# Inference step on one core: softmax factors in the turning matrix, compressed rows as one block, two landing places

## The chip, the cores and the metric

One Trainium2 chip, one of its cores. The metric is device microseconds (us) of one execution of the whole program; a kernel's time is the median of its runs. The profiled execution of the kernel before is one more execution of the same program, with its own time.

## The reference

One inference step of a small decoder with two trunk layers, for a prompt of 512 rows and a sample group of 8 rows (520 columns in the kernel). Layer 0 joins a state-space branch and an attention branch (16 heads of 64, two key groups) between one input projection and one output projection; layer 1 is a convolution module; behind each comes a feed-forward block. The change touches the attention of the prompt. For 128 queries and a head, three softmaxes are taken, each is scaled by a gate, and the weighted sums of the values are added:

```python
s_c = einsum('btghd,bngd->btghn', qg, kc)            # 31 compressed rows
p_c = masked_softmax(s_c, m_c);  o_c = einsum('btghn,bngd->btghd', p_c, vc)
p_s = masked_softmax(s_s, m_s);  o_s = einsum('btghnl,bgtnld->btghd', p_s, sel_v)   # selected blocks
p_w = masked_softmax(s_w, m_w);  o_w = einsum('btghs,bsgd->btghd', p_w, win_v)      # window
o = g[..., 0:1] * o_c + g[..., 1:2] * o_s + g[..., 2:3] * o_w
```

## The kernel before

Everything stands transposed: features on the 128 partitions, rows (tokens) along the free axis. Weights and activations are split into a high and a low fp32r part, and a product is three passes (mm3, L310): high by high, high by low, low by high. wload (L296) brings a weight tile of 128x1024 (512 KB) into a landing place, raw, by a DMA that SyncE issues; split (L292) makes its high part on ScalarE and its low part on VectorE, and the landing place is free again when the low part is made. The pool raw has three places, is opened once at the start (L264), and serves the whole program.

The mixer (L684) runs layer 0 in stages. First the projections of keys, values and queries and the whole attention of the sample group, with 10 of 40 tiles xz of the input projection for the state-space branch. Then the attention of the prompt: 16 steps (4 head groups hg of 4 heads, by 4 blocks b of 128 queries), between which the other 30 xz tiles are put. Then the scans of the four state-space groups, with the first 16 tiles of the output projection beside them, and at last the other 8 output tiles (wout(1, m)), which need the last scans' output.

A step of attention (L1106 to L1216) splits the queries into QS, makes the scores of the compressed rows (32 keys for each of the four heads, into pc) and their softmax, and for each head the scores over 128(b+1) keys twice (r = 0 the window, r = 1 the selected blocks), their maxima on VectorE and their exponentials on ScalarE, into pt. The sums give the factors mx[:, 2] (gate by reciprocal). L1174 to L1180 multiply each of the 8 exponentials of the step by its factor, in place: on VectorE, but r = 0 of b = 0 and b = 2 on ScalarE (ACT_NORM). Then turned (L1182) turns the weights: for each block of 128 keys and each r four transposes by the identity (L1186) into one PSUM tile pT of 512 columns, which is split into pth (ScalarE) and ptl (VectorE); two products of 512 columns by the block's values VB add into po (L1199, L1200). The compressed rows come last, as a block of 32 keys: four transposes of 32 columns, a split of 32x512, two products with VC. The tiles pT and po share three PSUM places (gen, L692); pth and ptl have two places each.

begin (L1653) closes layer 0: behind the last scan's pools (sp_, fx, ux, closed at L1446 to L1448) it opens the pools of what follows, h among them, which lie where the scan's tiles lay, and the last 8 output tiles use these pools and the landing places raw. The order of instructions on each engine is set by a planner from the program's order and its own estimate of durations; each engine works its list in that order.

## Time and profile before

| | us |
|---|---|
| median of 3 runs (lowest, highest) | 1958.77 (1958.25, 1962.19) |
| the profiled execution | 1961.67 |
| its span, first to last instruction | 1959.9 |
| attention of the prompt, first QS to the last sum, in the span | about 270 to 668 |
| last scan, boundary to the last 8 output tiles | about 845 to 905 |

In the profile, PE is TensorE's products and PEld its weight loads, which overlap; DVE is VectorE, ACT is ScalarE, POOL is GpSimd, SPq is SyncE's queue of DMA issues. A line of a group gives the kernel line, the engine, the operation, what it writes and reads, the tile shapes and how often it runs. PE's busy time counts pipelined products with modelled ends, so a product's own duration (about 0.27 us) is much longer than the distance to the next one; the rate of a run of products is read from starts. PEclk is the granted clock of TensorE as a share of 2.4 GHz.

### The profile page before, as it was taken

The page shows a single profiled execution, that of the slowest core. Times are in us where ns is not written, and L with a number is a line of the kernel's source. Part 1 is how long each engine was busy: PE and PEld are TensorE (multiplying, and loading weights), DVE is VectorE, ACT ScalarE, POOL GpSimd, SP SyncE. Part 2 cuts the span into 40 slices and gives each one's busy share as a digit, 9 for nine tenths or more (in the row PEclk, how much of TensorE's full clock was granted, in tenths as well). Part 3 has the DMA queues.
Part 4 walks back from the last instruction along what each step waited for, and adds up shares of the span by engine and source line. Part 5 has one row for each costly group of instructions (what it writes and reads, how often), then busy time and mean ns, then how long its engine had stood idle before and what let it go on. Part 6 is the DMA issues. An engine that isn't in the chain of part 4 may idle for free.

```text
span 1959.9 us, 38005 instructions
## 1 busy us (share of the span) xinstructions
PE 1835.2 (94%) x14449; PEld 1706.1 (87%) x14449; DVE 1415.3 (72%) x3385; ACT 974.4 (50%) x2093; POOL 189.5 (10%) x226
## 2 busy tenths in 40 slices
PE   6998889999998799998999999999989899999997
PEld 5997888988887588987999999998667789999997
DVE  5764768888887698968667766574786865666766
ACT  3223446676666577646555433355127755444433
POOL 0000021101000003130000211001111000000000
PEclk9999998999998799989999999999999999999999
DMA  8446254444321274543245433222433223444421
GB/s 296 114 140 197 76 190 130 149 138 129 126 90 57 92 243 136 157 143 100 87 143 165 132 105 109 87 81 53 119 107 119 87 87 116 122 119 120 148 62 49
DMA packets 125947, 240.90 MB, mean 123 GB/s; under 512 B 16499, under 2 KB 63236, under 8 KB 125444
## 3 DMA queue, kind: packets, MB, share of 16 engines
q1 hardware_dynamic: 120676, 221.45, 36.9%
q0 software_dynamic: 4000, 13.73, 2.2%
q10 hardware_dynamic: 1088, 3.29, 0.5%
q8 instruction: 114, 1.87, 0.4%
q14 instruction: 69, 0.57, 0.1%
HBM read 200.75 MB, written 30.88 MB: 118 GB/s over the span
## 4 chain that ended last, share of the span: by engine, by line
PE 43%; DVE 5%; ACT 3%; DMA 2%; issue 1%; SPq 0%; POOL 0%; DVEq 0%; ACTq 0%; POOLq 0%
PE up L312 8%; PE up L313 8%; PE up L314 8%; PE dn L312 4%; PE dn L313 4%; PE dn L314 4%; PE dn L624 2%; PE pw L312 1%; PE pw L313 1%; PE pw L314 1%; PE ns L333 1%; DMA raw_dn<-in_w_down 1%; DVE xf L385 1%; DVE h L387 1%; DVE facc L631 1%
## 5 line engine op out<-in xcount | busy, mean ns | idle before, releaser
L312 PE MATMUL dn<-gh,wh_dn 128*128 128x256 f32 (+1 forms) x704 | 198.0, 285 | 4.8 <-ACT gh L463 2.6
L314 PE MATMUL dn<-gh,wl_dn 128*128 128x256 f32 (+1 forms) x704 | 198.9, 284 | 0.0
L313 PE MATMUL dn<-gl,wh_dn 128*128 128x256 f32 (+1 forms) x704 | 198.4, 283 | 0.0
L451 DVE SCALAR_TENSOR_TENSOR c<-up,vec,c 128x511 f32<-128x511 f32 (+2 forms) x216 | 138.9, 645 | 16.1 <-ACT c L448 15.7
L312 PEld LDWEIGHTS dn<-gh,wh_dn 128*128 128x128 f32 x704 | 131.5, 189 | 6.8 <-DVE facc L478 3.7
L313 PEld LDWEIGHTS dn<-gl,wh_dn 128*128 128x128 f32 x704 | 133.1, 189 | 0.1
L314 PEld LDWEIGHTS dn<-gh,wl_dn 128*128 128x128 f32 x704 | 132.8, 189 | 0.0
L464 POOL TENSOR_TENSOR gl<-gm,gh 128x520 fp32r<-128x520 f32 (+2 forms) x54 | 61.8, 1145 | 700.6 <-ACT gh L463 700.5
L446 DVE TENSOR_TENSOR up<-up,rsx 128x520 f32<-128x520 f32 (+2 forms) x108 | 65.0, 603 | 81.5 <-PE up L314 79.9
L478 DVE TENSOR_TENSOR facc<-dn,facc 128x256 f32<-128x256 f32 (+1 forms) x160 | 66.2, 423 | 66.4 <-PE dn L314 66.1
L293 ACT ACTIVATE wh_up<-raw_up 128x1024 fp32r<-128x1024 f32 x68 | 72.0, 1058 | 71.8 <-PE up L313 46.5
L312 PE MATMUL acc<-x0hm,wh_xz 128*128 128x256 f32 x320 | 96.3, 301 | 6.9 <-ACT u L1001 4.5
L294 DVE TENSOR_TENSOR wl_up<-raw_up,wh_up 128x1024 fp32r<-128x1024 f32 x68 | 83.1, 1222 | 23.0 <-ACT wh_up L293 22.9
L314 PE MATMUL acc<-x0hm,wl_xz 128*128 128x256 f32 x320 | 94.3, 295 | 0.0
L313 PE MATMUL acc<-x0lm,wh_xz 128*128 128x256 f32 x320 | 94.1, 294 | 0.0
L313 PE MATMUL acc<-x1lm,wh_xz 128*128 128x264 f32 x320 | 92.8, 290 | 0.0
L312 PE MATMUL acc<-x1hm,wh_xz 128*128 128x264 f32 x320 | 92.6, 289 | 0.0
L448 ACT ACTIVATE c<-up,vec 128x520 f32<-128x520 f32 (+2 forms) x108 | 74.9, 695 | 34.8 <-DVE up L446 34.4
L314 PE MATMUL acc<-x1hm,wl_xz 128*128 128x264 f32 x320 | 92.1, 288 | 0.0
L293 ACT ACTIVATE wh_dn<-raw_dn 128x1024 fp32r<-128x1024 f32 (+1 forms) x48 | 47.4, 988 | 87.7 <-PE dn L313 62.8
L294 DVE TENSOR_TENSOR ptl<-pT,pth 128x512 fp32r<-128x512 f32 (+1 forms) x96 | 65.0, 684 | 25.8 <-ACT pth L293 25.6
L293 ACT ACTIVATE pth<-pT 128x512 fp32r<-128x512 f32 (+1 forms) x96 | 56.3, 595 | 53.1 <-PE pT L1186 49.9
(584 smaller groups left out, 6859.7 us busy)
## 6 DMA issues: line engine op xcount, KB each, us to landing
raw_up<-in_w_up SPq DMA_DIRECT2D x68, 512.0 KB, 3.8
raw_xz<-in_w_in SPq DMA_DIRECT2D x40, 512.0 KB, 4.8
raw_dn<-in_w_down SPq DMA_DIRECT2D x32, 512.0 KB, 3.7
raw_wo<-in_w_out SPq DMA_DIRECT2D x24, 512.0 KB, 4.2
raw_pw<-in_w_pw SPq DMA_DIRECT2D x24, 512.0 KB, 3.8
spill<-uth SPq DMA_DIRECT2D x40, 260.0 KB, 2.0
st<-in_st SPq DMA_DIRECT2D x40, 256.0 KB, 4.2
cc<-in_c_cmp SPq DMA_DIRECT2D x64, 128.0 KB, 2.6
```

What stands on the lines that cost most here:

```text
L293: nc.scalar.activation(hi, src, AF.Copy)
L294: (eng or nc.vector).tensor_sub(lo, src, hi.bitcast(F32))
L312: nc.tensor.matmul(ps, hi[:, wc], xh, start=first, stop=False)
L313: nc.tensor.matmul(ps, hi[:, wc], xl, start=False, stop=False)
L314: nc.tensor.matmul(ps, lo[:, wc], xh, start=False, stop=last)
L333: nc.tensor.matmul(ps, ones, acc[:, :n], start=i < group, stop=i == len(ks) - 1)
L446: nc.vector.tensor_mul(u(a, e0), u(a, e0), rv[:, a:e0])
L448: nc.scalar.activation(c[:, rs], u(r0, r1), AF.Identity, bias=V("fb", l * 44 + mt), scale=W(2, mt))
L451: nc.vector.scalar_tensor_tensor(c[:, a:e], u(a - d, e - d), W(2 - d, mt), c[:, a:e], op0=ALU.mult, op1=ALU.add)
L464: nc.gpsimd.tensor_sub(gl[:, rs], gm[:, rs], gh[:, rs].bitcast(F32))
L478: nc.vector.tensor_add(f, ps, f)
L624: nc.tensor.matmul(ps[i * 32:i * 32 + 32], cw[m][:, 4 * q + i], x4[m][:, i, cs], start=q == 0, stop=q == NQ[m] - 1)
```

## The change

Three edits:

- The 8 exponentials of a step are no longer multiplied by their factors. A tile dg of 128x1024 is made on VectorE from the identity and mx[:, 2]: eight diagonal matrices, one for each head and r. Each transpose of the exponentials becomes a plain f32 product of the same tile with its diagonal matrix.
- The compressed rows of the four heads are one block of 128 keys (4 heads by 32): one transpose, one split of 128x128, and for each head two products of 128 columns with VC, which now holds each head's 32 rows in its own partitions and zeros in the others. This block comes first in po. For it the values are made for 128 partitions, and VC is set to zero and filled by four splits.
- The mixer has a pool rawm of two landing places; begin opens a pool raw of three for what follows. The queries qh come by step (128x256, two places) instead of by head group (128x1024, one place), pc has one place instead of two.

```diff
-ACT_NORM = (0, 2)
-    P["raw"] = ctx.enter_context(tc.tile_pool(name="raw", bufs=3, side="right"))
-        VC = ap.tile([32, 2, 2, 64], F32R, name="VC")
+        VC = ap.tile([128, 2, 4, 2, 64], F32R, name="VC")
...
+                hid4 = tp.tile([128, 2, 4, 32], F32, tag="cc4", name="chid4", bufs=1)
+                nc.vector.tensor_copy(hid4, hid[:, :, None, :].to_broadcast([128, 2, 4, 32]))
                 for g in range(2):
-                    nc.tensor.matmul(ps[0:32, g * 64:g * 64 + 64], hid[:, g], w2[:, 128:192], start=True, stop=True)
...
+                    nc.tensor.matmul(ps[:, g * 64:g * 64 + 64], hid4[:, g].rearrange("p h c -> p (h c)"), w2[:, 128:192],
+                                     start=True, stop=True)
...
+                nc.vector.memset(VC.bitcast(F32), 0.0)
+                for hh in range(4):
+                    rw = slice(32 * hh, 32 * hh + 32)
+                    split(VC[rw, :, hh, 0], VC[rw, :, hh, 1], vc[rw])
...
-            qh = tp.tile([128, 2, S], F32, tag="qh", name="qh", bufs=1)
-            nc.sync.dma_start(qh, d_q[hg])
             for b in range(4):
...
+                qh = tp.tile([128, 2, 128], F32, tag="qh", name="qh", bufs=2)
+                nc.sync.dma_start(qh, d_q[hg][:, :, b * 128:b * 128 + 128])
...
-                pc = tp.tile([128, 4, 32], F32, tag="pc", name="pc", bufs=2)
+                pc = tp.tile([128, 4, 32], F32, tag="pc", name="pc", bufs=1)
...
+                dg = tp.tile([128, 4, 2, 128], F32, tag="dg", name="dg", bufs=1)
+                nc.vector.tensor_mul(dg.rearrange("p h r q -> p (h r) q"), ident[:, None, :].to_broadcast([128, 8, 128]),
+                                     mx[:, 2].rearrange("p h r -> p (h r)")[:, :, None].to_broadcast([128, 8, 128]))
+
+                def parted(pT):
+                    ph, pl = (tp.tile([128, 512], F32R, tag="pt" + p, name="pt" + p, bufs=THB)[:, :pT.shape[-1]]
+                              for p in "hl")
+                    split(ph, pl, pT)
+                    return ph, pl
...
+                pT = gen(128, "pT")
+                nc.tensor.transpose(pT, pc.rearrange("p h k -> p (h k)"), ident)
+                ph, pl = parted(pT)
                 for hh in range(4):
+                    for p in (ph, pl):
+                        nc.tensor.matmul(po[:, hh * 128:hh * 128 + 128], VC[:, g, hh].rearrange("p a d -> p (a d)"), p,
+                                         start=hh == 0 and p is ph, stop=False)
+                for n in range(b + 1):
                     for r in range(2):
-                        p = Ps[hh][:, r, 0:nw]
-                        if r == 0 and b in ACT_NORM:
-                            nc.scalar.activation(p, p, AF.Copy, scale=mx[:, 2, hh, r:r + 1])
-                        else:
-                            nc.vector.tensor_scalar(p, p, mx[:, 2, hh, r:r + 1], None, op0=ALU.mult)
...
+                        pT = gen(512, "pT")
+                        for hh in range(4):
+                            nc.tensor.matmul(pT[:, hh * 128:hh * 128 + 128], Ps[hh][:, r, n * 128:n * 128 + 128],
+                                             dg[:, hh, r], start=True, stop=True)
+                        ph, pl = parted(pT)
+                        v = VB[:, 1 - r, n, g].rearrange("p a d -> p (a d)")
+                        nc.tensor.matmul(po, v, ph, start=False, stop=False)
+                        last = nc.tensor.matmul(po, v, pl, start=False, stop=n == b and r == 1)
...
         P["fp"] = ctx.enter_context(tc.tile_pool(name="fp", bufs=1, space=PSUM))
+        P["raw"] = ctx.enter_context(tc.tile_pool(name="raw", bufs=3))
...
-    with tc.tile_pool(name="wum", bufs=3, side="right") as P["wu"]:
+    with tc.tile_pool(name="rawm", bufs=2, side="right") as P["raw"], \
+            tc.tile_pool(name="wum", bufs=3, side="right") as P["wu"]:
         new = mixer(begin)()
```

## Rows read from the trace of the kernel before

**Rows 1.** The page: busy time, share of the span, instructions, of each engine.

```profile
PE 1835.2 (94%) x14449; PEld 1706.1 (87%) x14449; DVE 1415.3 (72%) x3385; ACT 974.4 (50%) x2093; POOL 189.5 (10%) x226
```

**Rows 2.** Windows: length, busy of PE, PEld, DVE, ACT, POOL; clock, DMA, GB/s.

```profile
270.00:320.00 50.00, 42.85 (x314) 38.45 (x313) 38.24 (x169) 27.36 (x78) 6.25 (x12) 0.88 0.62 205
320.00:612.00 292.00, 284.15 (x2224) 258.85 (x2222) 247.41 (x766) 191.80 (x475) 24.50 (x34) 0.99 0.39 120
612.00:668.00 56.00, 46.81 (x182) 30.70 (x182) 39.24 (x111) 29.28 (x71) 0.00 (x0) 0.76 0.07 22
```

**Rows 3.** Waits of PE from 320 to 612: us in total, times, longest.

```profile
PE sc L1123 <- ACT pt L1169: 3.8, 5, 1.5
PE po L1199 <- ACT pth L293: 2.9, 3, 1.5
PE po L1200 <- DVE ptl L294: 1.1, 3, 0.5
```

**Rows 4.** Lines (busy us, mean ns) and one source line (min/median/max ns) on DVE and ACT.

```profile
L294 DVE TENSOR_TENSOR wl_xz<-raw_xz,wh_xz 128x1024 fp32r<-128x1024 f32 x40 | 48.8, 1219 | 7.7 <-ACT wh_xz L293 7.5
L1180 DVE TENSOR_SCALAR pt<-pt,mx 128x256 f32<-128x256 f32 (+3 forms) x96 | 31.1, 389 | 0.2
L1178 ACT ACTIVATE pt<-pt,mx x32: 384/522/617, 300.1 to 632.4; 128x128 f32<-128x128 f32 x16, 128x384 f32<-128x384 f32 x16
```

**Rows 5.** Transposes and f32 products of 128 columns: source lines, and runs in the timeline.

```profile
L1186 PE MATMUL pT<-cst,pt x320: 270/272/476, 302.9 to 662.8; 128*128 128x128 f32 x160
L936 PE MATMUL cmpAB<-cc,w x512: 272/275/377, 61.0 to 214.2; 128*128 128x128 f32 x171
...
662.45 0.60 PE L1186 MATMUL pT<-cst,pt 128*128 128x128 f32 x4
...
101.10 2.62 PE L936 MATMUL cmpAB<-cc,w 128*128 128x128 f32 x22
```

**Rows 6.** Timeline of PE: narrow fp32r products, and a product of 512 columns.

```profile
309.00 0.26 PE L1124 MATMUL sc<-KL,QS 128*128 128x32 f32 x1
309.11 0.26 PE L1123 MATMUL sc<-KH,QS 128*128 128x32 f32 x1
...
662.11 0.50 PE L1200 MATMUL po<-ptl,VB 128*128 128x512 f32 x1
```

**Rows 7.** Timeline of the last step, from the factors to the last sum.

```profile
648.19 0.20 DVE L1172 RECIPROCAL mx<-mx 128x8 f32<-128x8 f32 x1 [0.31 <-ACT pt L1169]
...
652.99 0.60 ACT L293 ACTIVATE pth<-pT 128x512 fp32r<-128x512 f32 x1 [3.94 <-PE pT L1186]
...
665.03 0.68 DVE L294 TENSOR_TENSOR ptl<-pT,pth 32x512 fp32r<-32x512 f32 x1 [0.62 <-ACT pth L293]
...
665.76 0.18 PEld L1200 LDWEIGHTS po<-ptl,VC 32*128 32x128 f32 x1 [0.53 <-DVE ptl L294]
```

**Rows 8.** Timelines at the boundary; last two: windows of tile acc (length, PE, PEld).

```profile
844.98 0.38 SPq L302 DMA_DIRECT2D raw_wo<-in_w_out  x1
...
863.39 1.35 SPq L1658 DMA_DIRECT2D h<-in_x  x2
863.39 2.96 ACT L293 ACTIVATE wh_wo<-raw_wo 128x1024 fp32r<-128x1024 f32 x3 [1.51 <-POOL x1ls L294]
874.05 1.06 ACT L293 ACTIVATE wh_wo<-raw_wo 128x1024 fp32r<-128x1024 f32 x1 [7.70 <-DMA raw_wo<-in_w_out]
...
856.80:863.40 6.60, 6.24 (x22) 5.13 (x23) 0.41 (x1) 0.00 (x0) 0.50 0.00 0
863.40:875.20 11.80, 11.39 (x93) 11.19 (x93) 1.62 (x4) 0.00 (x0) 0.98 0.88 311
```

**Rows 9.** Page and timelines: landing of output weights; loads of the first query weights.

```profile
raw_wo<-in_w_out SPq DMA_DIRECT2D x24, 512.0 KB, 4.2
...
11.14 0.73 SPq L302 DMA_DIRECT2D raw_q<-in_w_in  x1
23.26 0.34 SPq L302 DMA_DIRECT2D raw_q<-in_w_in  x1
```

More of the change, by code (lines that the diff above doesn't have):

```diff
@@ L751, in mixer @@
         w2 = tp.tile([128, 192], F32, name="w2", bufs=1)
-        b2v = tp.tile([64, 128], F32, name="b2v", bufs=1)
+        b2v = tp.tile([128, 128], F32, name="b2v", bufs=1)
         pe = tp.tile([128, 2, 2, 8], F32, name="pe", bufs=1)
@@ L906, in mixer @@
             else:
+                hid4 = tp.tile([128, 2, 4, 32], F32, tag="cc4", name="chid4", bufs=1)
+                nc.vector.tensor_copy(hid4, hid[:, :, None, :].to_broadcast([128, 2, 4, 32]))
                 for g in range(2):
[L908 to L912 removed]
+                    nc.tensor.matmul(ps[:, g * 64:g * 64 + 64], hid4[:, g].rearrange("p h c -> p (h c)"), w2[:, 128:192],
+                                     start=True, stop=True)
+                vc = tp.tile([128, 2, 64], F32, tag="ub", name="vcP", bufs=2)
+                nc.vector.scalar_tensor_tensor(vc.rearrange("p g d -> p (g d)"), ps, 0.5, b2v, op0=ALU.mult, op1=ALU.add)
+                nc.vector.memset(VC.bitcast(F32), 0.0)
+                for hh in range(4):
+                    rw = slice(32 * hh, 32 * hh + 32)
+                    split(VC[rw, :, hh, 0], VC[rw, :, hh, 1], vc[rw])
         qs = tp.tile([128, KD, NB], F32, name="qs", bufs=1)
@@ L1173, in attention @@
                 nc.vector.tensor_mul(mx[:, 2], mx[:, 2], gTsw[:, b, 4 * hg:4 * hg + 4])
-                for hh in range(4):
-                    for r in range(2):
-                        p = Ps[hh][:, r, 0:nw]
-                        if r == 0 and b in ACT_NORM:
-                            nc.scalar.activation(p, p, AF.Copy, scale=mx[:, 2, hh, r:r + 1])
-                        else:
-                            nc.vector.tensor_scalar(p, p, mx[:, 2, hh, r:r + 1], None, op0=ALU.mult)
-                def turned(ps4, kn):
-                    pT = gen(512, "pT")
-                    for hh in range(4):
-                        nc.tensor.transpose(pT[0:kn, hh * 128:hh * 128 + 128], ps4[hh], ident)
-                    ph, pl = (tp.tile([128, 512], F32R, tag="pt" + p, name="pt" + p, bufs=THB)[0:kn] for p in "hl")
-                    split(ph, pl, pT[0:kn])
+                dg = tp.tile([128, 4, 2, 128], F32, tag="dg", name="dg", bufs=1)
@@ L1192, in attention @@
                 po = gen(512, "po")
-                parts = [(VB[:, 1 - r, n, g], [p[:, r, n * 128:n * 128 + 128] for p in Ps], 128)
-                         for n in range(b + 1) for r in range(2)]
-                parts.append((VC[:, g], [pc[:, hh] for hh in range(4)], 32))
-                for k, (v, ps4, kn) in enumerate(parts):
-                    ph, pl = turned(ps4, kn)
-                    v = v.rearrange("p a d -> p (a d)")
-                    nc.tensor.matmul(po, v, ph, start=k == 0, stop=False)
-                    last = nc.tensor.matmul(po, v, pl, start=False, stop=k == len(parts) - 1)
+                pT = gen(128, "pT")
@@ new lines, in attention @@
+                nc.tensor.transpose(pT, pc.rearrange("p h k -> p (h k)"), ident)
[5 more added lines that the diff above has]
+                for n in range(b + 1):
+                    for r in range(2):
+                        pT = gen(512, "pT")
+                        for hh in range(4):
+                            nc.tensor.matmul(pT[:, hh * 128:hh * 128 + 128], Ps[hh][:, r, n * 128:n * 128 + 128],
[4 more added lines that the diff above has]
+                        last = nc.tensor.matmul(po, v, pl, start=False, stop=n == b and r == 1)
```

10 lines of the change are left out of this document (3 added, 7 removed).

## The prediction

> **What bounds the kernel now.** I read the page first: TensorE is busy for 94% of the span, so the question is where it is not, and whether the change works there [rows 1]. Then the windows over the attention of the prompt, which is where the first two edits act. It falls in three parts [rows 2]: from 270 to 320 TensorE is busy 42.85 of 50 us; from 320 to 612, where the xz tiles lie between the steps, 284.15 of 292; from 612 to 668, where these tiles have run out, 46.81 of 56 at a mean clock of 0.76 (the clock has two levels, 1.2 and 2.4 GHz, so about half of this part runs at the lower). In the middle part all waits of PE's products come to 7.8 us [rows 3], and VectorE is busy 247.41 of 292. So the middle is bound by TensorE, with VectorE at 85% close behind; the last part is a chain from step to step (factors, turned weights, split, sum), and a product more costs there only what the chain sees of it. PE's busy time has modelled ends, and the weight loads leave more room: 292 less 258.85, that is 33 us. The true slack of the middle lies between 8 and 33 us.
>
> **The normalising.** Removed are 96 instructions on VectorE, 31.1 us, and 32 on ScalarE at about 0.52, 16.6 us. Added is dg, 16 instructions on VectorE of 1024 elements from two tensors; the nearest row of that shape, wl_xz, takes 1.22 us, so 19.5 us [rows 4]. VectorE gains 11.6 us and ScalarE 16.6 us over the stage. Neither is the bound of the middle, and the waits of PE that hang on them are those 7.8 us [rows 3].
>
> **The turning.** A transpose is one instruction in the trace: 320 calls, 320 rows; four of them in a run last 0.60 us, so they start every 0.11 us (0.60 less one duration of 0.27, by three). A plain f32 product of 128x128 by 128 columns is two: compress makes 256 calls at L936 and the trace has 512 rows, and 22 rows in a run last 2.62 us, again 0.11 apart [rows 5]. So each of the 320 products costs TensorE 0.22 us where the transpose cost 0.11, and the change adds 320 instructions of 0.11: 36 us. Some 240 of them, those of three of the four head groups, fall in the middle part: 27 us. Against that stands a slack of 8 to 33 us, so the price there is 0 to 27. I take the 8 us of PE's row as used up and 2 us more for the lighter VectorE and ScalarE: 27 - 8 - 2 = 17. The row of PE is nearer than that of PEld, since the waits by name in it (7.8 us) are all there is to win, and they are for exponentials and splits, which this edit does not shorten.
> In the first part 24 products more, 2.7 us, go into 7 idle us: 0. In the last part the chain decides, seen at the last step [rows 7]: from the factors at 648.19 the first split starts at 652.99. Eight normalisings at 0.39 become one dg of 1.22, 1.9 us less. The compressed block no longer closes the step, 0.68 + 0.50 or 1.2 us less. Each of 8 blocks gets four more passes of 0.11; pT has two places beside po, so half of that shows up to all of it: 1.8 to 3.5 us more. That is between -1.3 and +0.4 for a step; I take 0, with -4 to +4 for the three steps.
> The Trainium skill (TensorE: Matmul & The Clock Gate, Terms) says that the transpose mode is four times faster for FP32. The rows above say two at this width. By the page the added time would be three transposes each, 106 us instead of 36; it is a rival below.
>
> **The compressed block.** Four transposes (0.44 us) and two products of 512 columns (about 0.22 each by the 0.34 between starts less the gap of a transpose, 0.11) become one transpose and eight products of 128 columns: 0.88 us against 0.11 + 8 x 0.11 = 0.99. The 0.11 is what fp32r products of 32 columns are apart [rows 6]; no row has 128 columns, so the upper bound is the 0.22 of two passes, 0.9 us more for a step. Over 16 steps +2 us, up to +16. The value is the row of 32 columns, which has the same weight load. The split of 512 columns becomes one of 128 and is hidden.
>
> **The landing places, at the boundary.** This is the part that is not about attention. In the kernel before, raw stands beside everything, and five of the last eight output weights are asked for before the boundary, the last of them at 844.98 [rows 8]. What begin opens can be filled only when the scan's tiles are read for the last time: h is asked for at 863.39, and ScalarE, though idle, starts the first weight into a new pool at 863.39 too, released by x1ls [rows 8]. The new raw is opened in begin, behind h, over the scan's tiles. So all eight weights now wait until 863.4, and with them SP's queue, in which h and the loads of the next stage stand. Before, TensorE had made 22 + 93 output products by 875.2 [rows 8], and 93 in 11.8 us is 0.127 each. If h's two loads go first, as the code has them, the first weight comes when the ones asked for behind h did, 874.05, and is ready at 875.1: TensorE is 115 x 0.127 = 14.6 us behind. If a weight goes first, it lands 4.2 us after 863.4 [rows 9] and is split by 868.7, by when 22 + 42 products had been made: 8.1 us. I take 13, nearer to the code's order. Nothing hides it: the products that follow keep TensorE busy, and the feed-forward block starts from their sums.
> Within the mixer two places are enough for most of the time: the weights of xz and wo are asked for ten us and more ahead of use. At the start the third load went at 11.14 and the fourth at 23.26, when the first place was free [rows 9]; with two places the third goes at 23.26 and the fourth some 12 us later, and the page gathers behind them on SP's queue with it. Also VC's zeros and four splits come in here. I take 1 us, 0 to 8.
>
> **Edits at nothing.** The queries by step are 16 smaller loads on SP's queue, each waiting for the split of two steps before; behind one stand weights asked for long before use. dg has one place, so the next dg waits for this step's last product, but the next factors come later than that anyway, because pt has 5 places and the next exponentials wait for this step's turning. If the planner puts dg ahead of splits on VectorE's list, they wait with it; 0 to 3 us.
>
> **The sum.** 17 + 0 + 2 + 13 + 1 = 33 us. The profiled execution has 1961.67 us, 1.8 outside its span of 1959.9, and would become 1994.7; it lies 2.9 us (0.15%) above the median of 1958.77, so the median becomes 1991.8, say 1992. With the parts all at one end (middle 0 to 27, last part -4 to 4, compressed 2 to 16, boundary 8 to 15, start 0 to 8) it would be 1965 or 2029; as independent spreads (root of the squares) they leave 18 down and 19 up, 1974 to 2011 for this case.
>
> **Rivals.**
> Faster, 0.08: the chain sets the pace of the middle too, and TensorE's free 33 us are real. Then the normalising leaves the chain (-11.6 us) and the compressed block no longer closes a step (16 x 1.2, -19 us), and with +14 for the loads it is 1942. For it speaks that each step's factors come only when the step before has been turned; against it that PE's waits sum to 7.8 us. It decides from the point where 27 us of products find room in the weight loads' slack.
> No boundary cost, 0.12: the new raw is filled before 863.4, because the planner finds tiles that are free earlier, or the wait falls on work that is late anyway: 1992 - 13 = 1979.
> Clock, 0.08: the clock stands at 0.76 in the last part and 0.88 in the first, which is 13 and 6 us lost at most [rows 2]. TensorE is thin there while it waits, and products of twice the passes make it less thin; if half of that came back it is 1982. The Trainium skill (TensorE: Matmul & The Clock Gate, Part 4) says that transposes do not count as busy for the clock in the way products do, which would be the reason; no row here parts the two.
> Narrow products and a late start, 0.10: 128 columns at 0.22 (+14) and the start at +6: 2012.
> Four passes, 0.02: 960 passes of 0.11 are 106 us, three quarters in the middle, less 10: 69 + 16, or 2044. Rows 5 speak against it.
> The slack takes all and the boundary costs little, 0.05: within 0.2%.
>
> **How the numbers follow.** My forecast has 0.55, and the predicted time is its value. It leaves 0.08 faster, 0.05 the same and 0.87 slower; 0.2% is about what a measurement of this kernel can tell from no change. The range takes in the forecast's own bounds and the rivals at 1979, 1982 and part of 2012, and leaves out the faster case, four passes and the far ends: 1968 to 2012.
>
> **What would show it.** The middle part's share of PE stays near 97% while it gets longer by 15 to 20 us, L1186's place shows 640 rows, and ptl no longer waits for normalising. At the boundary no raw_wo is asked for in the 20 us before the last x1ls, and PE idles behind it for 8 us or more with DMA as the releaser. I am wrong if the stage of the attention is shorter than 398 us, or if weights land before the scan's last read.

## The result, and the profile after

The changed kernel takes 1989.45 us (median of 4 runs, 1984.07 to 1993.86) against 1958.51 us (1956.22 to 1962.19). The ratio on record is 1.0149, 95% interval 1.0127 to 1.0171 (the two medians alone give 1.0158). The forecast was 1992.0 us in a range of 1968 to 2012. Number and sign held. Several terms behind the number did not, and the experiments show that their errors cancelled, which is luck.

The profiled execution of the changed kernel is its longest, 1993.86 us, with a span of 1992.1. The page's line of busy times, beside [rows 1]:

```profile
PE 1853.6 (93%) x14817; PEld 1751.3 (88%) x14817; DVE 1407.4 (71%) x3310; ACT 964.8 (48%) x2066; POOL 185.8 (9%) x226
```

TensorE has 368 instructions more (320 second passes, the rest from the compressed block); VectorE is 8 us lighter and ScalarE 10. The windows that answer to [rows 2], with the same columns, the waits of PE from 320 to 612 ([rows 3]), and dg from 320 to 612 and its products in the whole stage (line, engine, operation and tiles, count, busy us, mean ns):

```profile
270.00:320.00 50.00, 44.72 (x348) 42.22 (x347) 37.44 (x156) 26.52 (x73) 5.31 (x10) 0.90 0.63 200
320.00:612.00 292.00, 286.91 (x2371) 273.71 (x2370) 232.15 (x705) 175.21 (x437) 20.55 (x34) 1.00 0.37 114
612.00:668.00 56.00, 50.34 (x314) 45.13 (x313) 35.74 (x90) 28.92 (x74) 0.00 (x0) 0.88 0.16 51
...
PE po L1207 <- DVE ptl L292: 4.0, 3, 1.6
PE po L1206 <- ACT pth L291: 1.0, 1, 1.0
...
L1179 DVE TENSOR_TENSOR dg<-cst,mx 128x1024 f32<-128x1024 f32 x11 | 13.5, 1223 | 0.5
L1202 PE MATMUL pT<-dg,pt 128*128 128x128 f32 x640 | 90.1, 287 | 3.6 <-DVE dg L1179 3.6
```

The fixed windows are fuller in all three stretches. They do not show how much longer the stage is, because its end has moved. The next view cuts the stage at the starts of three events of its own: the first query split (QS), the last tanh of an xz tile, the last otmp of the attention. Windows of before and then of after, same columns:

```profile
269.60:612.50 342.90, 327.89 (x2540) 297.96 (x2539) 286.55 (x935) 220.06 (x555) 30.75 (x46) 0.98 0.42 132
612.50:666.30 53.80, 44.94 (x171) 29.30 (x171) 37.77 (x106) 28.19 (x69) 0.00 (x0) 0.75 0.07 22
```

```profile
266.90:635.20 368.30, 357.93 (x2922) 341.66 (x2920) 288.12 (x908) 217.89 (x554) 27.95 (x48) 0.99 0.40 125
635.20:673.90 38.70, 32.77 (x169) 26.98 (x169) 21.94 (x52) 16.45 (x38) 0.00 (x0) 0.82 0.09 28
```

The part with xz tiles between the steps grew by 25.4 us, and the tail without them shrank by 15.1: the planner lets the tiles last 22.7 us longer, so fewer steps are left without cover (two steps end in the tail, four before). The attention as a whole went from 396.7 to 407.0, +10.3.

The boundary after, in the timeline (start, length, engine, instruction; in brackets the idle time before it and the releaser), and then windows of the products of tile acc, as in [rows 8]:

```profile
815.02 0.33 SPq L300 DMA_DIRECT2D raw_wo<-in_w_out  x1
...
869.53 1.33 SPq L1665 DMA_DIRECT2D h<-in_x  x2
870.92 19.19 SPq L300 DMA_DIRECT2D raw_wo<-in_w_out  x8
...
879.80 1.06 ACT L291 ACTIVATE wh_wo<-raw_wo 128x1024 fp32r<-128x1024 f32 x1 [11.75 <-DMA raw_wo<-in_w_out]
...
880.91 0.58 PE L310 MATMUL acc<-x0hs,wh_wo 128*128 128x256 f32 x1 [17.90 <-ACT wh_wo L291]
...
869.50:880.90 11.40, 0.00 (x0) 0.00 (x0) 0.00 (x0) 0.00 (x0) 0.50 0.91 310
880.90:886.40 5.50, 5.46 (x24) 5.15 (x25) 0.00 (x0) 0.00 (x0) 0.50 0.66 216
886.40:898.20 11.80, 11.80 (x98) 11.67 (x97) 1.26 (x3) 0.00 (x0) 1.00 0.77 231
```

No output weight is asked for between 815.02 and 870.92. All eight come behind h, and TensorE waits 17.90 us for the first. Then 24 products run at a granted clock of 0.50. From the scans' last x1ls to the last output product it is 43.9 us before and 66.0 after. Two more rows bear on this: products of tile acc in before, ahead of the window in [rows 8], and a wait of PE in after that comes later (what waited, for what: us, times, longest; 840 to 920).

```profile
847.80:851.20 3.40, 3.31 (x23) 2.91 (x24) 0.00 (x0) 0.00 (x0) 1.00 0.73 273
...
PE acc L310 <- DVE facc L1287: 3.2, 3, 2.4
```

All kernels are compared by the same events below: **start** up to the first QS, **attention** (with xz tiles + tail) to the last otmp, **scans** to the end of the last x1ls, **boundary** to the last output product, **rest** to the end of the span. The columns in us are from one profiled execution each; median and ratio (with its 95% interval) are from the timed runs. Each ratio is to runs of the kernel before that stand beside that set of experiments, whose median was 1959.1 us for e1 to e4, 1960.2 for e5 to e8 and 1961.6 for e9 to e12, so it is not the quotient of two rows, and medians of different sets can differ by about 3 us for this reason alone. One execution of e8 took 2055.2 us at a mean clock of 0.833 and is left out of its median.

The last column splits the attention into three. Idle is its length less PE's busy time. Clock is half of the time that the granted clock stood at 0.50 in it: half, because products take about twice as long there (24 in 5.5 us at 0.50, 98 in 11.8 us at 1.00, in the windows above). Work is the rest, TensorE's products as at full clock. Where TensorE idles at the lower clock, time is counted twice, so work is an estimate that can be up to 4 us low.

| kernel | median | ratio to before | start | attention | scans | boundary | rest | attention: idle + clock + work |
|---|---|---|---|---|---|---|---|---|
| before | 1958.5 | | 269.6 | 396.7 (342.9 + 53.8) | 197.1 | 43.9 | 1052.6 | 23.9 + 22.2 + 350.6 |
| after | 1989.5 | 1.0149 [1.0127, 1.0171] | 266.9 | 407.0 (368.3 + 38.7) | 195.6 | 66.0 | 1056.6 | 16.3 + 11.9 + 378.8 |
| e1_b_land | 1986.8 | 1.0140 [1.0113, 1.0168] | 276.6 | 394.7 (343.0 + 51.7) | 194.6 | 65.1 | 1054.1 | 25.6 + 17.1 + 352.0 |
| e2_a_keep | 1983.3 | 1.0120 [1.0094, 1.0146] | 268.4 | 406.6 (368.8 + 37.8) | 197.6 | 51.6 | 1053.7 | 16.4 + 11.9 + 378.3 |
| e3_a_turn | 1965.2 | 1.0028 [1.0014, 1.0043] | 266.7 | 381.5 (335.6 + 45.9) | 196.0 | 66.9 | 1053.0 | 19.2 + 13.6 + 348.7 |
| e4_b_prod | 1985.6 | 1.0135 [1.0107, 1.0162] | 269.0 | 414.5 (371.1 + 43.4) | 196.4 | 43.5 | 1058.5 | 17.0 + 10.2 + 387.3 |
| e5_best | 1950.5 | 0.9954 [0.9940, 0.9969] | 267.9 | 376.5 (331.4 + 45.1) | 200.9 | 43.1 | 1057.9 | 16.4 + 8.6 + 351.5 |
| e6_best_dg | 1963.7 | 1.0023 [1.0010, 1.0035] | 267.2 | 401.9 (369.2 + 32.7) | 199.9 | 43.4 | 1054.1 | 14.2 + 8.5 + 379.2 |
| e7_best_r | 1956.9 | 0.9989 [0.9972, 1.0007] | 264.6 | 390.2 (353.2 + 37.0) | 197.3 | 42.9 | 1057.6 | 23.0 + 23.9 + 343.3 |
| e8_b_qstep | 1951.6 | 0.9967 [0.9951, 0.9984] | 268.1 | 395.6 (333.9 + 61.7) | 192.7 | 43.3 | 1050.1 | 23.9 + 18.7 + 353.0 |
| e9_no_factor | 1928.3 | 0.9830 [0.9802, 0.9857] | 267.4 | 363.9 (342.9 + 21.0) | 199.2 | 43.5 | 1051.9 | 13.1 + 5.1 + 345.7 |
| e10_ones_pass | 1934.0 | 0.9859 [0.9834, 0.9885] | 267.3 | 364.1 (342.4 + 21.7) | 195.6 | 42.0 | 1059.6 | 12.0 + 6.9 + 345.2 |
| e11_last | 1969.9 | 1.0045 [1.0026, 1.0064] | 265.4 | 406.9 (320.5 + 86.4) | 196.0 | 42.0 | 1057.5 | 30.9 + 23.9 + 352.1 |
| e12_old_block | 1974.4 | 1.0076 [1.0051, 1.0101] | 272.6 | 396.9 (343.8 + 53.1) | 197.3 | 44.3 | 1060.2 | 25.4 + 18.8 + 352.7 |

Scans and rest differ by up to 8 and 10 us between kernels whose code there is the same or differs only in where weights land. No experiment takes these differences apart, so a difference of medians holds more than the stage that was edited. Where one stage is judged, its own column is used.

The last column says what the change did to the attention: work +28.2 us, idle -7.6, clock -10.3. TensorE has more to do, and part of it comes back as less idle time and less time at the lower clock.

### The profile page after: what moved, and what is told of

It is laid out like the page before. It is cut to its first block, busy times and chain, and to the rows that moved or that the text cites. A ratio compares the mean times of both kernels' runs of the same rounds, so it can differ in the third digit from the quotient of the medians.

```text
span 1992.1 us, 38666 instructions
## 1 busy us (share of the span) xinstructions
PE 1853.6 (93%) x14817; PEld 1751.3 (88%) x14817; DVE 1407.4 (71%) x3310; ACT 964.8 (48%) x2066; POOL 185.8 (9%) x226
## 3 DMA queue, kind: packets, MB, share of 16 engines
q10 hardware_dynamic: 1152, 3.32, 0.5%
## 4 chain that ended last, share of the span: by engine, by line
PE 43%; DVE 5%; ACT 3%; DMA 3%; issue 1%; SPq 1%; DVEq 0%; ACTq 0%
PE up L310 7%; PE up L311 7%; PE up L312 7%; PE dn L310 4%; PE dn L311 4%; PE dn L312 4%; PE dn L622 2%; PE pw L311 1%; PE pw L312 1%; PE pw L310 1%; DMA raw_dn<-in_w_down 1%; PE ns L331 1%; DVE xf L383 1%; DMA raw_wo<-in_w_out 1%; ACT wh_dn L291 1%
## 5 line engine op out<-in xcount | busy, mean ns | idle before, releaser
L462 POOL TENSOR_TENSOR gl<-gm,gh 128x520 fp32r<-128x520 f32 (+2 forms) x54 | 61.7, 1143 | 704.1 <-ACT gh L461 704.0
L1202 PEld LDWEIGHTS pT<-dg,pt 128*128 128x128 f32 x640 | 86.9, 202 | 7.6 <-DVE dg L1179 4.4
L1202 PE MATMUL pT<-dg,pt 128*128 128x128 f32 x640 | 90.1, 287 | 3.6 <-DVE dg L1179 3.6
L446 ACT ACTIVATE c<-up,vec 128x520 f32<-128x520 f32 (+2 forms) x108 | 74.8, 694 | 30.4 <-DVE up L444 29.9
```

The costliest lines, as they stand in the source:

```text
L446: nc.scalar.activation(c[:, rs], u(r0, r1), AF.Identity, bias=V("fb", l * 44 + mt), scale=W(2, mt))
L462: nc.gpsimd.tensor_sub(gl[:, rs], gm[:, rs], gh[:, rs].bitcast(F32))
L1202: nc.tensor.matmul(pT[:, hh * 128:hh * 128 + 128], Ps[hh][:, r, n * 128:n * 128 + 128], dg[:, hh, r], start=True, stop=True)
```

## Experiments on the boundary

**e1_b_land**: the landing edit alone, on the kernel before (the first line added stands in begin).

```
-    P["raw"] = ctx.enter_context(tc.tile_pool(name="raw", bufs=3, side="right"))
...
+        P["raw"] = ctx.enter_context(tc.tile_pool(name="raw", bufs=3))
...
+    with tc.tile_pool(name="rawm", bufs=2, side="right") as P["raw"], \
```

> The kernel before with the landing edit alone: two places inside the mixer, three new ones opened in begin; the attention is as before. My theory: all eight last output weights wait for the scan's last read, TensorE falls 13 to 22 us behind at the boundary and gets nothing back, so 1972 to 1981 us; the stage of the attention keeps its 397 us. Rival, two places are too few inside the mixer: the loss is already there at the last read of the scan (x1ls later than 863 by 5 us or more). Rival, no cost of the boundary (the 22 us between the traces come from the later attention): 1958 to 1961.

The boundary took 65.1 us, 21.2 more than before, with the attention at 394.7. The wait of TensorE (what waited, for what: us, times, longest; 840 to 920):

```profile
PE acc L311 <- ACT wh_wo L292: 17.9, 1, 17.9
```

It is the same 17.9 us as in the changed kernel: the boundary's loss belongs to this edit alone. The total was 27.6 us beside its own set's before, above my theory's 13 to 22; in the trace the start also came 7.0 us later. The scans' last read came 2.5 us later than before, not the 5 or more of the rival of two places.

**e2_a_keep**: the changed kernel, with the last eight output weights in the mixer's two places.

```
-            return wload(I["w_out"][kg, m], 1, "wo", tag)[0]
+            return wload(I["w_out"][kg, m], 1, "wo", tag, "rm" if kg == 1 else "raw")[0]
```

> The kernel after, with the last eight output weights landing in the mixer's two places, which are there before begin; the new places of begin serve the weights behind them. My theory: the boundary's wait goes, so 1989 less 13 to 22, or 1967 to 1976 us, and the attention stays at its 407 us. Rival, the boundary's loss is that of two places as such: 1985 or more, with DMA still the releaser of TensorE there. Rival, downstream drift is a cost of its own (places of begin lying lower): the end comes 10 us less early than the last output product does.

The boundary fell to 51.6 us, 14.4 back of 22. The timeline of SP's queue shows why not all:

```profile
844.66 0.33 SPq L300 DMA_DIRECT2D raw_wo<-in_w_out  x1
...
853.79 0.37 SPq L300 DMA_DIRECT2D raw_wo<-in_w_out  x1
...
872.65 1.33 SPq L1665 DMA_DIRECT2D h<-in_x  x2
874.03 2.60 SPq L300 DMA_DIRECT2D raw_us<-in_w_up  x3
876.73 0.91 SPq L300 DMA_DIRECT2D raw_wo<-in_w_out  x2
...
886.47 3.08 SPq L300 DMA_DIRECT2D raw_us<-in_w_up  x3
...
890.74 1.46 SPq L300 DMA_DIRECT2D raw_wo<-in_w_out  x2
```

Two places let four of the eight weights go early (two of the requests are shown). Of the others two stand in the queue behind h and three weights of the next stage, and two behind six. The median, 1983.3, moved by 6 us only and missed my 1967 to 1976; medians and profiles differ by what the table's other columns do.

**e6_best_dg**: the changed kernel with two more places opened ahead of the scans, beside which there is room, and one in begin.

```
         P["fa"] = ctx.enter_context(tc.tile_pool(name="fa", bufs=1))
+        P["r2"] = ctx.enter_context(tc.tile_pool(name="raw2", bufs=2))
+        P["land"] = itertools.cycle((P["raw"], P["r2"]))
...
-        P["raw"] = ctx.enter_context(tc.tile_pool(name="raw", bufs=3))
+        P["r1"] = ctx.enter_context(tc.tile_pool(name="raw1", bufs=1))
```

> The kernel after with the landing changed alone: two places inside the mixer, two more opened ahead of the scans, one in begin. My theory: the stretch from the scan's last read to the last output product falls from 66 us to 44 or so, the rest stays, so 1989.5 less 22, or 1965 to 1970 us. Rival, the boundary hides part of it behind other late work, as the 6 us between the medians of the run with two kept places say: 1980 or more.

The boundary is 43.4 us, as before the change, and the median 1963.7, 25.7 below the changed kernel and just under my 1965 to 1970. SP's queue around it:

```profile
852.24 0.56 SPq L300 DMA_DIRECT2D raw_wo<-in_w_out  x1
...
869.01 1.33 SPq L1668 DMA_DIRECT2D h<-in_x  x2
...
872.12 1.38 SPq L300 DMA_DIRECT2D raw_wo<-in_w_out  x2
```

Only two weights are left behind h, and the 17.9 us wait is gone. Shown: the loss at the boundary is the wait of the weights for places over the scan's tiles. Two places that are there before h give 14.4 of the 22.1 us back (e2), four give all of it (e6), so the number of early places counts too. The rival that part of it hides behind other work falls.

## Experiments on the factors

**e3_a_turn**: the factors back on the exponentials, and transposes by the identity, all else as changed.

```
-                dg = tp.tile([128, 4, 2, 128], F32, tag="dg", name="dg", bufs=1)
...
+                for hh in range(4):
+                    for r in range(2):
+                        p = Ps[hh][:, r, 0:nw]
...
-                            nc.tensor.matmul(pT[:, hh * 128:hh * 128 + 128], Ps[hh][:, r, n * 128:n * 128 + 128],
-                                             dg[:, hh, r], start=True, stop=True)
+                            nc.tensor.transpose(pT[:, hh * 128:hh * 128 + 128], Ps[hh][:, r, n * 128:n * 128 + 128], ident)
```

> The kernel after with the softmax factors back on the exponentials (96 instructions on VectorE, 32 on ScalarE) and the turning back to transposes by the identity, so 320 passes fewer; compressed block and landing as in after. My theory: the attention loses 10 to 17 us of its 407 and the time goes to 1972 to 1979. Rival, the compressed block or the queries by step are what made the attention longer: it stays at 403 us or more and the time at 1985 to 1990. Rival, the lighter VectorE was worth more than the passes cost: the time rises above 1992.

1965.2 us, and the attention took 381.5: 25.5 less than with dg, more than my 10 to 17. And it is 15.2 less than the kernel before, though it has the landing edit in it. Something else in the change makes the attention shorter, which my forecast does not have.

**e4_b_prod**: the kernel before, with the 320 transposes made plain f32 products by the identity.

```
-                        nc.tensor.transpose(pT[0:kn, hh * 128:hh * 128 + 128], ps4[hh], ident)
+                        if kn == 128:
+                            nc.tensor.matmul(pT[:, hh * 128:hh * 128 + 128], ps4[hh], ident, start=True, stop=True)
+                        else:
+                            nc.tensor.transpose(pT[0:kn, hh * 128:hh * 128 + 128], ps4[hh], ident)
```

> The kernel before with one thing changed: the 320 transposes of the exponentials are plain f32 products by the identity, which is 320 instructions more on TensorE; factors stay on the exponentials, compressed block and landing as before. My theory: 240 of them in the part bound by TensorE at 0.11 us are 27 us, less the free 8 to 10: 1975 to 1978 us; all of them seen would be 36, or 1994. Rival, the weight loads' slack of 33 us takes them: 1958 to 1962. Rival, the price is in the waits of dg and not in the passes: under 1963.

1985.6, 26.4 above before; the attention 414.5, +17.8. The part with xz tiles grew by 28.2 us and the tail shrank by 10.4, the pattern of the changed kernel. The slack of the weight loads took nothing: work is up by 36.7 us, all 36 of the passes, while idle is 6.9 less and clock 12.0 less. The rest of the difference is behind the attention (5.9 us in the rest).

**e7_best_r**: e6 with dg and the exponentials in fp32r, so each product is one pass.

```
-                    pt = tp.tile([128, 2, 512], F32, tag="pt", name="pt", bufs=5)
+                    pt = tp.tile([128, 2, 512], F32R, tag="pt", name="pt", bufs=5)
...
-                dg = tp.tile([128, 4, 2, 128], F32, tag="dg", name="dg", bufs=1)
+                dg = tp.tile([128, 4, 2, 128], F32R, tag="dg", name="dg", bufs=1)
```

> The last kernel with dg and the exponentials rounded to fp32r, so that each of the 320 products is one pass. If the second pass is the whole price of putting the factors into the matrix, the attention falls from 407 to 381 us or below (the 31 and 17 us of normalising stay away): 1938 to 1946 us. Rival, an fp32r product of 128 columns by a 128x128 weight takes two passes' time: as with dg in f32, 1965 to 1970. Rival, dg's own place in the chain is part of the price: 390 us or more of attention, 1950 or more.

The attention took 390.2 us: of 25.4 between e5 and e6 the second passes gave back 11.7. Work fell by 35.9 us, the whole price of the passes, but idle rose by 8.8 and clock by 15.4. The rival with dg's own price held. In the part with xz tiles PE's waits on the splits are longer than without dg (waits of PE from first QS to last xz tile, e7 and then e10 below, which has no factors):

```profile
PE sc L1126 <- ACT pt L1172: 5.4, 4, 1.8
PE po L1207 <- DVE ptl L292: 4.8, 5, 2.6
PE po L1206 <- ACT pth L291: 3.3, 2, 2.3
```

```profile
PE sc L1129 <- ACT pt L1175: 3.7, 3, 1.9
PE po L1207 <- DVE ptl L292: 2.5, 2, 1.7
```

And the longest waits go with a loss of clock. One of them, in the timeline of PE and in windows (columns as in [rows 2]):

```profile
377.21 0.51 PE L1207 MATMUL po<-ptl,VB 128*128 128x512 f32 x1 [2.63 <-DVE ptl L292]
...
377.20:379.00 1.80, 1.79 (x13) 1.65 (x13) 1.77 (x11) 0.00 (x0) 0.55 (x1) 1.00 1.01 391
379.00:382.40 3.40, 3.40 (x18) 3.40 (x18) 3.31 (x16) 1.61 (x3) 0.55 (x1) 0.51 0.55 168
```

Four such stretches, of 3.4 to 6.8 us, lie in e7's middle, beside waits of 2.63, 1.06, 0.99 and 2.27 us. A wait of about 1 us need not do this: e7 has another of 1.34 us (at 536.76), and the changed kernel four of 0.96 to 1.61, with no such stretch beside them. From first QS to last xz tile the clock stood at its lower level for 30.7 us in e7 and for 10.2 in e5, e6, e10 and the changed kernel. Half of the 20.5 between them is 10 us; that part is 10.8 longer in e7 than in e10 (353.2 against 342.4), with 44 rows fewer in it, so the two need not match.

The windows of the two parts, e7 and then e10, carry this to the whole stage:

```profile
264.60:617.80 353.20, 336.18 (x2639) 316.97 (x2638) 282.77 (x899) 210.95 (x547) 27.24 (x48) 0.96 0.41 129
617.80:654.80 37.00, 31.04 (x133) 24.57 (x132) 23.42 (x60) 18.21 (x43) 0.00 (x0) 0.77 0.05 15
```

```profile
267.30:609.70 342.40, 333.10 (x2683) 316.40 (x2683) 274.55 (x909) 217.62 (x562) 26.86 (x48) 0.99 0.43 133
609.70:631.40 21.70, 18.95 (x91) 13.63 (x91) 14.25 (x37) 12.09 (x28) 0.00 (x0) 0.92 0.05 19
```

By the table's last column the 26.1 us between them are 11.0 of idle and 17.0 of clock, and none of TensorE's work.

**e9_no_factor** and **e10_ones_pass**: e5 without the normalising, and e7 with the identity in dg's place.

```
-                        if r == 0 and b in ACT_NORM:
-                            nc.scalar.activation(p, p, AF.Copy, scale=mx[:, 2, hh, r:r + 1])
-                        else:
-                            nc.vector.tensor_scalar(p, p, mx[:, 2, hh, r:r + 1], None, op0=ALU.mult)
```

```
+        idr = tp.tile([128, 128], F32R, name="idr", bufs=1)
+        nc.vector.tensor_copy(idr, ident)
...
-                                             dg[:, hh, r], start=True, stop=True)
+                                             idr, start=True, stop=True)
```

> The best kernel so far with the 96 + 32 normalising instructions left out and nothing in their place, so the softmax factors are left out of the result: transposes by the identity, no dg. It shows what the lighter VectorE and ScalarE are worth by themselves. Theory A, they are worth what the forecast counted (2 us in the middle, 1.9 for each step of the last part): attention 368 to 373 us against 376.5, time 1942 to 1947. Theory B, TensorE bounds all but a few steps and they are worth nothing: 375 to 378 us, 1949 to 1952. Theory C, the chain of a step runs through them everywhere: 16 steps by 2 to 3 us, under 345 us, below 1920.

> The run with one pass for each product, with the identity (rounded to fp32r) in the place of dg, so the softmax factors are left out of the result; otherwise the same 320 fp32r products on rounded exponentials. That run had 390 us of attention, where the second pass was to be the whole price (381 or less). If waiting for dg is the rest of the price, it goes here and the attention is within 2 us of the run without factors. If the fp32r products or the rounding of the exponentials cost more than transposes, it stays at 386 us or more, 1953 to 1960.

Without factors both take 364 us of attention (363.9 and 364.1), so an fp32r product of 128 columns and a transpose cost the same. The factors cost 12.6 us as normalising (e5 less e9) and 26.1 as dg (e7 less e10). By the medians it is 22 and 23 us (24 each, if each is first set against the kernel before of its own set); the difference lies outside the attention, in stages that are not edited. What both readings say is that dg, 1.22 us on VectorE in place of eight instructions, is not the cheaper way to put the factors in. Theory A had 3.5 to 8.5 us for the normalising, which is too low: taking it away is worth more than I had counted. What fell is that dg keeps this gain. Its price is idle time and clock, by the column above; why putting dg in leads to so many more waits is open. It can be dg's own single place or the order that the planner makes around it: no run has two places for dg (there is no room), and none holds the order fixed.

## Experiments on the compressed block, the queries and the best version

**e12_old_block**: e5 with the compressed block as in the kernel before (its lines are in the diff of the change, with a minus).

> The best kernel so far with the compressed block undone: four transposes, a split of 512 columns and two products with 32 rows at the end of each step; the queries by step and the landing places stay. It is the kernel before with queries by step and the new landing. Theory, the compressed block is what shortened the attention: attention 394 to 397 us and the time 1950.5 plus 15 to 20, or 1953 (the run with queries by step) if the landing places cost nothing: so 1953 to 1970, by the attention 15 us above that of the best kernel. Rival, the landing places shortened the attention: 380 us or less.

Attention 396.9 us, 20.4 above e5; median 1974.4, 24 above and over the 1953 to 1970 that I expected. The compressed block is what shortened the attention, against my forecast of +2. One price that I had wrong is in the trace of before. Timeline of PE there, around the two products of a compressed block:

```profile
408.01 0.28 PE L313 MATMUL acc<-x1lm,wh_xz 128*128 128x264 f32 x1
408.23 0.49 PE L1199 MATMUL po<-pth,VC 32*128 32x512 f32 x1
408.65 0.39 PE L314 MATMUL acc<-x1hm,wl_xz 128*128 128x264 f32 x1
408.88 0.28 PE L312 MATMUL acc<-x1hm,wh_xz 128*128 128x264 f32 x1
409.00 0.28 PE L313 MATMUL acc<-x1lm,wh_xz 128*128 128x264 f32 x1
```

and after, the new ones:

```profile
409.99 0.28 PE L1196 MATMUL po<-pth,VC 128*128 128x128 f32 x1
410.10 0.28 PE L1196 MATMUL po<-ptl,VC 128*128 128x128 f32 x1
410.21 0.28 PE L1196 MATMUL po<-pth,VC 128*128 128x128 f32 x1
```

The starts tell the price. A product with 32 rows and 512 columns holds the engine for 0.42 us (408.23 to 408.65, and the median of all 32), where one with 128 rows and 512 columns takes 0.24 (median of the 160 products with VB in before). The two starts beside it are 0.22 and 0.23 apart, where its neighbours are 0.12 apart. So each of the 32 costs about 0.42 + 0.1 + 0.1 = 0.6 us, and not 0.22. The eight new ones are 0.11 apart, as forecast; the new transpose costs 0.11 to 0.17, with the wider start behind it. That is 32 x 0.6 + 64 x 0.11 = 26 us before against 16 x 0.15 + 128 x 0.11 = 16 after, an estimate of 10 us of TensorE's time.

The stage does not show that much. The windows of the two parts, e5 and then e12:

```profile
267.90:599.30 331.40, 322.34 (x2593) 301.05 (x2593) 280.90 (x935) 217.29 (x558) 26.96 (x48) 0.98 0.44 137
599.30:644.40 45.10, 37.72 (x178) 25.64 (x179) 35.27 (x104) 25.82 (x63) 0.00 (x0) 0.92 0.05 15
```

```profile
272.60:616.40 343.80, 329.61 (x2545) 298.67 (x2543) 285.59 (x937) 218.68 (x558) 32.48 (x47) 0.98 0.43 131
616.40:669.50 53.10, 41.87 (x165) 27.68 (x165) 36.54 (x101) 27.81 (x65) 0.00 (x0) 0.81 0.04 13
```

By the table's last column the old block costs 9.0 us more idle and 10.2 more clock, and work differs by 1.2 (5 at most, with what is counted twice). So most of the 20.4 us are waits and the clock that goes with them, and not the price of the products.

**e11_last**: e5 with the new compressed block moved back to the end of the step.

```
-                pT = gen(128, "pT")
-                nc.tensor.transpose(pT, pc.rearrange("p h k -> p (h k)"), ident)
-                ph, pl = parted(pT)
...
                 for n in range(b + 1):
...
+                pT = gen(128, "pT")
+                nc.tensor.transpose(pT, pc.rearrange("p h k -> p (h k)"), ident)
+                ph, pl = parted(pT)
...
```

> The best kernel so far with the compressed block put back to the end of each step, as in the kernel before; its one transpose and eight products are unchanged. My forecast counted 1.2 us for each step of the last part for its place: three steps, attention 376.5 plus 3 to 5 us, 1953 to 1956. Rival, the place is what made the attention 15 to 20 us shorter than before: 390 us or more, 1964 or more. Rival, only the cheaper products count: 1949 to 1952.

The attention took 406.9 us, 30.4 more than e5 and 10 more than the old block in the same place. Work is the same to 0.6 us; idle is 14.5 more and clock 15.3. So the cheaper products alone do not bring the gain. But this run is not a clean price of the place: with the block last, the planner used up the xz tiles by 585.9, and the tail without them is 86.4 us. What is shown is that the gain is not there with the block last. How much of the 20 us comes from the chain, where the block's products no longer close a step, and how much from the order that the planner makes with it, these runs do not tell.

**e8_b_qstep**: the kernel before with the queries loaded by step.

```
-            qh = tp.tile([128, 2, S], F32, tag="qh", name="qh", bufs=1)
-            nc.sync.dma_start(qh, d_q[hg])
...
+                qh = tp.tile([128, 2, 128], F32, tag="qh", name="qh", bufs=2)
+                nc.sync.dma_start(qh, d_q[hg][:, :, b * 128:b * 128 + 128])
```

> The kernel before with the queries loaded by step and not by head group, and nothing else. My forecast put this at nothing: 1958 to 1960 us, attention 395 to 399 us. Rival, it is where the 15 us of attention come from that the run with the factors back gained against the kernel before: 1943 to 1950. Rival, it brings the attention's start forward (269.6 us in before, 266.9 in after, 276.6 with the landing edit alone): first QS at 262 us or earlier.

1951.6 us, 3 to 10 us below before by the interval of the ratio: not nothing. The trace does not put it in one place: start -1.5, attention -1.1, scans -4.4, rest -2.5. It is not the 15 us of e3.

**e5_best**: e3 with the landing places of e6.

> The factors back on the exponentials, transposes by the identity, compressed block and queries by step as in after; the landing changed: two places inside the mixer, two more opened ahead of the scans, and for the feed-forward blocks these two and one opened in begin. My theory from the runs so far: the attention keeps the 381 us of the run with the factors back, and the boundary's 22 us go, so 1965 less 15 to 22, or 1943 to 1950 us, 0.5 to 0.8% faster than the kernel before. Rival, the boundary's loss is two places fewer as such or h's loads, and not the wait for the scan's last read: the last output product still comes 60 us or more after the scan's last read and the time is 1960 or more.

1950.5 us, 0.5% faster than before (0.3 to 0.6%) and 39 us faster than the change. It keeps the compressed block, the queries by step and more room, and drops dg. The boundary is 43.1 us and the attention 376.5. Its gain is half of what the attention gives (20 us): scans and rest are 3.8 and 5.3 us longer in its profile.

## Why the prediction was right, and where it was not

By the trace the change costs -2.7 at the start, +10.3 in the attention, -1.5 in the scans, +22.1 at the boundary and +4.0 in the rest: 32.2 us, where the sum had 33. Term by term:

- **The bound of the middle: right.** TensorE is busy 286.91 of 292 us after, and the waits that I counted as slack shrank from 7.8 to 5.0. The rival in which the weight loads' slack takes the passes fell in e4.
- **The turning: price right, place and size wrong.** 640 rows stand at L1202, 0.112 apart. The forecast fixed the parts at 320 and 612 us and put three quarters of the passes in the middle. In the kernel the xz tiles move with the work: between e5 and e6 the part under xz tiles has 327 rows more and is 37.8 us longer, that is all 36 us of passes and not 27, and the tail, which I held at 0, is 12.4 us shorter because it has fewer steps. Net the edit costs 25 us and not 17. In TensorE's work the passes cost their full 36 us in the two comparisons that change little else in the attention (e4 36.7, e6 to e7 35.9); what the kernel pays is less where idle time and clock shrink beside them.
- **The lighter VectorE: wrong sign, because dg's own price was put at nothing.** I took 2 us off in the middle and 1.9 for each late step, and listed dg's one place among the edits at nothing, with 0 to 3 us. e9 says that taking the normalising away is worth 12.6 us; e7 and e10 say that dg costs 26.1, in idle time and clock. In the last step of e7 the first split does come sooner after the reciprocal than in e5, as forecast (2.4 against 3.9 us in the timelines), but the eight splits of that step follow at wider distances at a lower clock (0.70 from 638 to 655 in e7, 0.80 from 628 to 645 in e5), and nothing is left of it.
- **The compressed block: wrong sign, the largest error.** I forecast +2, bounded by 2 and 16, and it is -15 (e3) to -20 (e12). Two steps failed. The block's place at the end of a step was counted for three steps; the -19 for all sixteen stood only in the rival that ended faster, and most of the measured gain is idle time and clock (19.2 of 20.4 us in e12). And the product of 32 rows was priced like one of 128, from a gap between [rows 6] and [rows 5], though its own rows were in the trace; that is worth 10 us by the starts and 1 to 5 by the sums of the stage.
- **The boundary: mechanism right in each step, mis-sized.** The weight behind h came into use 11.4 us after the last x1ls, where I had 11.7 (863.4 to 875.1). But I priced the delay as 115 products at 0.127, 14.6 us, and took 13. Three things were missing. Before had made 24 more of these products already, in a window ahead of the one I counted in (847.80 to 851.20, above): of the 1152 output products it had made 814 by the end of the last x1ls, and after had made 768, 46 fewer. By 11.4 us behind that end before had made 133 of the 384 products of the last eight weights; at 0.12 each that is 16.0 us. After then pays for a lower clock once more (24 products in 5.5 us, 2.6 more than at 0.12 each). And further on it waits 3.2 us for VectorE's sums (facc, above), where before waited 0.8. Together that is 16.0 + 2.6 + 2.4 = 21.0 of the 22.1. The 8.1 of the other order did not occur.
- **The start: +1 forecast, -2.7 measured.** The landing edit alone costs 7.0 there (e1), as the range had it (0 to 8), and together with the queries by step 3.0 (e12); with the new compressed block beside them the start is early. Why is open.
- **The clock rival was part of the result.** Clock lost in the attention, by the two windows of each kernel: 342.9 x 0.02 + 53.8 x 0.25 = 20 us before, 368.3 x 0.01 + 38.7 x 0.18 = 11 after. So 9.6 us came back, the rival's figure, 6.5 of them in the tail, which is shorter and less of it at the lower clock. This lies inside the stage's +10.3 and not beside it. e4, where only the transposes became products, loses 12.0 us less clock than before; from e5 to e6, which has the same exchange with dg, clock stays as it was. So what gave the clock back is open. The Trainium skill (TensorE: Matmul & The Clock Gate, Part 4) would have it come from transposes turned into products. e9 and e10, the one with transposes and the other with as many products of one pass, have the same mean clock, 0.978, and 10.2 and 13.7 us at the lower clock in the attention, so no run here shows that.
- **The transpose's factor.** The Trainium skill (TensorE: Matmul & The Clock Gate, Terms) has the transpose mode four times faster for FP32. At 128 columns it is two here: 640 rows 0.112 us apart for dg against 320 rows 0.109 apart for the transposes in e3.

So the forecast was right that its two named losses are there, 22 and 25 us where it had 13 and 17, and the 17 us by which it was short were made up by the compressed block for the most part (it was to cost 2 us, and e3, which has the queries by step in it too, is 15 below before). That the sum still met the measured time is luck.

## What to carry to other kernels

Before an operation is made wider or narrower, take its price from the starts of its own rows, of just that number of rows and columns; the nearest other shape was off by a factor of two to three here. In a stage where a planner fills gaps with other work, cut the trace at events and not at times: the filler moves, and a cost in the full part comes back in the part where the filler has run out. When a stage changes its length, split the difference into idle time, clock and work before a price is given to an instruction: the block's products look 10 us cheaper by their starts, and the 20 us that it saved are nearly all idle time and clock. A place for data that is opened over tiles still being read is a wait for their last reader, and whatever is queued behind its load waits too.

## What the runs showed of the hardware

- In before the next instruction starts 0.42 us after an fp32r product of 512 columns with 32 rows (median of 32, nearly all standing between products of 128 rows) and 0.24 us after one with 128; beside a 32-row product the starts are 0.1 us wider. Its own length in the trace is 0.49 us against 0.40. The Trainium skill (TensorE: Matmul & The Clock Gate, Why this matters for your kernels) gives a single product with K=32 the time of K=128; the trace does not agree.
- In e7 TensorE idled for 1 to 2.6 us in an otherwise full stage, four times, and each time the granted clock went to 0.5 (1.2 GHz) for 3.4 to 6.8 us, in the wait or within 2 us of its end. A fifth wait of 1.34 us there, and four of 0.96 to 1.61 us in the changed kernel, had no such stretch beside them.
- Plain f32 products of 128 columns are two rows of 0.11 us; the same in fp32r is one row of 0.111 (e7, e10), and a transpose one of 0.109.
